# Other first loads, eleven products of zeros, one part per step at the start, and thirteen unread products before the feed-forward, in a one-layer decoder step

## The chip, the core and the metric

The kernel runs on one core of a Trainium2 chip. The metric is the device time of one execution in microseconds (us); lower is better. The engines meant below are TensorE (PE in the profile; its weight loads stand apart as PEld), VectorE (DVE), ScalarE (ACT), GpSimd (POOL) and the queue of SyncE (SP), which issues most of the transfers. A name such as ACTq or SPq is an engine's queue issuing a transfer.

## What is computed

One layer of a hybrid decoder over 288 token columns (256 of a prompt, 8 sequences of 4 new tokens), in fp32:

```python
h = _rmsnorm(x, norm_pre_mix)
z = h @ w_in                                   # 2048 -> 8480
ya, new_wkv = _rwkv7_branch(zs_mix, st_wkv, ...)
yb, new_pool = _pool_branch(zp, st_pool, pos0, pool_w, pool_scale)
m = sigmoid(zga) * (ya @ w_branch_a) + sigmoid(zgb) * (yb @ w_branch_b)
x = x + _rmsnorm(m @ w_out, norm_post_mix)
f, new_conv = _conv_ffn(_rmsnorm(x, norm_pre_ffn), ...)   # 2048 -> 2*5632 -> 2048
x = x + _rmsnorm(f, norm_post_ffn)
```

`_rmsnorm` divides each token's row by the root of its mean square and multiplies by a gain per channel.

## The kernel before

Activations lie with channels on the 128 partitions and the 288 tokens along the free dimension, so x is 16 tiles `xr` of 128x288. Every large product is made of three TensorE products in a fast 32-bit form (`three`, L262 to L265): the weights are split into a rounded part `whi` (a copy on ScalarE, L202) and the rest `wlo` (a subtraction on VectorE, L203), the activation into `xh` (ScalarE, L356) and `xl` (VectorE, L357), and hi·xh, hi·xl and lo·xh are added up in one PSUM bank. A **unit** is 128 output channels by 512 input channels of weights, one 256 KB load into one of seven `raw` buffers; it feeds 4 x 3 = 12 products. `whi` and `wlo` have four buffers each. `take` splits three units ahead of the one it hands out and loads six further.

**The beginning.** The RMS norm is not applied to x first: the products run on x times the gain, and the token's factor `rstd_mix` is multiplied in when a PSUM bank is read. The first group (`dense_together`, list `seq_lo`) works on five outputs at a time, one of them 96 channels wide: for each of four quarters of the input channels, five units, so 20 units and 240 products; units 0 to 4 need `xh` and `xl` of tiles 0 to 3, units 5 to 9 those of tiles 4 to 7, and so on. `startup` is a generator that runs beside it on a lane, one step per unit: it makes the parts of tiles 4 to 15, squares all tiles on ScalarE (`acc`, `sq`, L409 and L412), adds the squares on GpSimd (L413), and ends with `rstd_of`: a product with a tile of ones (L371), a square root and a reciprocal. `vec` holds all per-channel vectors (331 columns, gain g1 in the first 16), `con` the constants (1115 columns, with `ident`, `ones` and `bones`).

**The turn.** After the last of the 16 outputs of w_out, `rstd_spread` forms the norm of the mixed branch: six products with two columns of ones each (L384), a square root (L389), a reciprocal (L390), a diagonal tile (L392) and one product that spreads the factor over all partitions (L396). Then `second_parts` makes the new x tile by tile (L1229, L1230) and its parts, and the first three gate/up pairs of the feed-forward (`dense_by_k`, six outputs at a time) start, one tile k at a time in the first quarter and two at a time later. `rstd_spread` is called a second time at the end of the program, there with products for the residual sum in its pauses.

**What sets the order.** The program is recorded in the order of the code and then put into an order per engine by a scheduler that runs its own model of the engines' times; every engine executes its list strictly in that order. `pin` fixes an instruction's place among the pinned ones. A change in one place can therefore move instructions in others.

## Time and profile before

| | |
|---|---|
| median of 3 runs | 1649.15 us (1648.79 to 1650.57) |
| the profiled execution | 1651.69 us |
| its span, first to last instruction | 1649.6 us |
| mean granted TensorE clock | 0.992 |
| TensorE busy | 1611.8 us, 13540 products |
| VectorE, ScalarE, GpSimd busy | 1103.4, 816.8, 369.7 us |

The profile is of one execution. Its page gives busy times and the chain of work that ended last; the trace behind it answers by group of instructions, by wait (who stood still until whom), by time and by stretch of time (busy time of each engine, granted clock, transfer rate). "PE acc L263 <- ACT whi L202: 8.8, 1, 8.8" reads: TensorE's product of L263 waited for ScalarE's `whi` of L202, 8.8 us in all, once, 8.8 us the longest. In a timeline row stand start, length, engine, line, operation, out<-in, how many in a row, and in brackets the idle time before it and what ended that.

### The profile page before, as it was taken

The numbers are of one execution on the slowest core, as the hardware profiler recorded it, in microseconds if no ns is written. First come the engines' busy times: TensorE is split into PE (matmuls) and PEld (weight loads), VectorE is DVE, ScalarE is ACT, GpSimd is POOL, SyncE is SP. The second block draws the span as 40 slices with busy tenths as digits, with TensorE's granted clock in tenths as the row PEclk, the third lists the DMA queues.
The fourth block names the chain that finished last, engine by engine and source line by source line (L and its number), as shares of the span: only waits on it lengthen the run. The fifth ranks groups of instructions, "written<-read, shape, count | busy, mean of one in ns | idle before, by whom it ended". The sixth has DMA issues, their size and how long they took to land.

```text
span 1649.6 us, 35997 instructions
## 1 busy us (share of the span) xinstructions
PE 1611.8 (98%) x13540; PEld 1577.3 (96%) x13540; DVE 1103.4 (67%) x2217; ACT 816.8 (50%) x1521; POOL 369.7 (22%) x612
## 2 busy tenths in 40 slices
PE   6989999999999999999999999999999999999998
PEld 6989989989989999999899999999999999999998
DVE  6788887888878766645876664446666555666654
ACT  5544445445435445545655554445555433455554
POOL 4574352343332112300211110001111000111111
PEclk9999999999999999999999999999999999999999
DMA  7535546546545648755355555555555555555553
GB/s 241 161 120 165 170 142 200 161 122 190 157 155 181 187 155 288 229 166 190 108 163 167 167 165 167 166 167 165 168 167 166 166 166 167 166 167 167 176 167 108
DMA packets 157230, 278.96 MB, mean 169 GB/s; under 512 B 25584, under 2 KB 32240, under 8 KB 157056
## 3 DMA queue, kind: packets, MB, share of 16 engines
q1 hardware_dynamic: 151104, 259.16, 50.8%
q0 software_dynamic: 5664, 16.77, 2.9%
q8 instruction: 106, 1.74, 0.4%
q10 hardware_dynamic: 288, 0.74, 0.1%
q14 instruction: 68, 0.56, 0.1%
HBM read 262.67 MB, written 13.93 MB: 168 GB/s over the span
## 4 chain that ended last, share of the span: by engine, by line
PE 86%; DVE 4%; DMA 2%; issue 1%; POOL 0%; ACT 0%; SPq 0%; DVEq 0%; POOLq 0%; ACTq 0%
PE acc L265 27%; PE acc L263 27%; PE acc L264 27%; DVE wlo L203 1%; DMA dW<-wt 1%; PE ps_g L671 0%; DVE xl L357 0%; DVE og L1229 0%; PE ps_s L909 0%; DMA W<-dW 0%; PE ps_u L899 0%; PE ps_x L888 0%; PE ps_y L1353 0%; DVE cum L577 0%; DMA raw<-in_w_in 0%
## 5 line engine op out<-in xcount | busy, mean ns | idle before, releaser
L203 DVE TENSOR_TENSOR wlo<-raw,whi 128x512 fp32r<-128x512 f32 x928 | 661.1, 715 | 415.2 <-ACT whi L202 406.7
L202 ACT CAST whi<-raw 128x512 fp32r<-128x512 f32 x928 | 572.0, 620 | 680.6 <-PE acc L264 629.7
L263 PE MATMUL acc<-xh,whi 128*128 128x288 f32 x2736 | 814.3, 298 | 14.5 <-ACT whi L202 8.8
L265 PE MATMUL acc<-xh,wlo 128*128 128x288 f32 x2736 | 811.4, 297 | 7.0 <-DVE wlo L203 7.0
L264 PE MATMUL acc<-xl,whi 128*128 128x288 f32 x2736 | 812.7, 297 | 0.0
L263 PEld LDWEIGHTS acc<-xh,whi 128*128 128x128 f32 x2736 | 517.4, 189 | 17.9 <-ACT whi L202 9.2
L265 PEld LDWEIGHTS acc<-xh,wlo 128*128 128x128 f32 x2736 | 520.2, 190 | 12.0 <-DVE wlo L203 8.9
L264 PEld LDWEIGHTS acc<-xl,whi 128*128 128x128 f32 x2736 | 520.6, 190 | 2.0 <-issue 0.9
L265 PE MATMUL acc<-ah,wlo 128*128 128x288 f32 x704 | 208.7, 296 | 0.0
L263 PE MATMUL acc<-ah,whi 128*128 128x288 f32 x704 | 208.0, 296 | 0.0
L264 PE MATMUL acc<-al,whi 128*128 128x288 f32 x704 | 205.2, 292 | 0.0
L1266 POOL COPY cout<-gt 128x2 f32<-128x2 f32 x44 | 31.1, 706 | 597.2 <-DVE gt L1262 575.9
L264 PEld LDWEIGHTS acc<-al,whi 128*128 128x128 f32 x704 | 134.2, 191 | 0.0
L263 PEld LDWEIGHTS acc<-ah,whi 128*128 128x128 f32 x704 | 132.2, 188 | 0.0
L265 PEld LDWEIGHTS acc<-ah,wlo 128*128 128x128 f32 x704 | 131.9, 187 | 0.0
L1274 POOL TENSOR_TENSOR cv<-cv,rstd_ffn 128x288 f32<-128x288 f32 x44 | 36.2, 823 | 74.5 <-ACT cv L1273 73.6
L732 DVE TENSOR_TENSOR wt<-wt,Ab 128x16 f32<-128x16 f32 (+30 forms) x124 | 51.4, 414 | 1.8
L462 POOL TENSOR_TENSOR df<-zt 128x256 f32<-128x256 f32 (+1 forms) x27 | 22.7, 840 | 91.6 <-DVE zt L460 85.6
L1270 DVE SCALAR_TENSOR_TENSOR cv<-gt,vec,cv 128x255 f32<-128x255 f32 x88 | 43.0, 489 | 0.0
L263 PE MATMUL acc<-ybh,whi 128*128 128x288 f32 x128 | 38.6, 301 | 0.0
L265 PE MATMUL acc<-ybh,wlo 128*128 128x288 f32 x128 | 38.4, 300 | 0.0
L264 PE MATMUL acc<-ybl,whi 128*128 128x288 f32 x128 | 38.1, 298 | 0.0
(308 smaller groups left out, 1539.8 us busy)
## 6 DMA issues: line engine op xcount, KB each, us to landing
raw<-in_w_ffn_in SPq DMA_DIRECT2D x352, 256.0 KB, 3.0
raw<-in_w_in SPq DMA_DIRECT2D x264, 256.0 KB, 3.5
raw<-in_w_ffn_out SPq DMA_DIRECT2D x176, 256.0 KB, 2.7
raw<-in_w_out SPq DMA_DIRECT2D x64, 256.0 KB, 3.0
raw<-in_w_branch_b SPq DMA_DIRECT2D x32, 256.0 KB, 3.2
raw<-in_w_branch_a SPq DMA_DIRECT2D x32, 256.0 KB, 3.9
xr<-in_xT SPq DMA_DIRECT2D x8, 288.0 KB, 5.6
tga<-th POOLq DMA_DIRECT2D x16, 144.0 KB, 3.7
```

What stands on the lines that cost most here:

```text
L202: act.copy(out=hi[:, a:b, :m], in_=w[:, a:b, :m])
L203: dve.tensor_tensor(lo[:, a:b, :m], w[:, a:b, :m], hi[:, a:b, :m].bitcast(F32), op=ALU.subtract)
L263: pe.matmul(ps, hi, xh, start=start, stop=False)
L264: pe.matmul(ps, hi, xl, start=False, stop=False)
L265: pe.matmul(ps, lo, xh, start=False, stop=stop)
L462: pool.tensor_tensor(df[:m, :TP], zt[:m, 0:TP], zt[:m, 1:ZB], op=ALU.subtract)
L732: dve.tensor_tensor(tmp[:, :, :n], Wb[:, :, :n], Ab[:, :n, tt].unsqueeze(1).to_broadcast([P, 8, n]), op=ALU.mult)
L1266: pool.tensor_copy(cout[:, f, 0:2], gt[:, TP - 2:TP])
L1270: dve.scalar_tensor_tensor(cv[:, s:TP], gt[:, 0:TP - s], w, cv[:, s:TP], op0=ALU.mult, op1=ALU.add)
L1274: pool.tensor_tensor(cv, cv, rst3, op=ALU.mult)
```

## The change

Three things change at the beginning. The ScalarE queue now loads only the 16 columns of g1; the other 315 columns of `vec` and all of `con` are issued on the SP queue just before the load of unit 7. The first load of x brings one tile instead of two, then come unit 0, the second tile, and tiles 2 and 3. `startup` makes one tile's parts and one square per step, in pinned order of the squares. GpSimd zeroes a 128x128 tile, and eleven products of this tile with itself (plain fp32, `ps_warm`, read by nobody) stand first on TensorE. At the turn `rstd_spread` gets five products of `ones` with `ident` (`ps_busy`, read by nobody) behind the sums and eight behind the spreading product. `bones_r`'s copy is pinned. The second call of `rstd_spread` is as before.

```diff
+WARM = 11
@@ load_to
+            if i == 7:
+                nc.sync.dma_start(out=vec[:, KD:], in_=t["vec"][:, KD:])
+                nc.sync.dma_start(out=con, in_=t["con"])
@@
-    nc.scalar.dma_start(out=vec, in_=t["vec"])
+    nc.scalar.dma_start(out=vec[:, 0:KD], in_=t["vec"][:, 0:KD])
...
-    nc.scalar.dma_start(out=con, in_=t["con"])
@@ x_load
-            nc.sync.dma_start(out=xq[:, 0:2], in_=t["xT"][:, 0:2, :])
+            nc.sync.dma_start(out=xq[:, 0:1], in_=t["xT"][:, 0:1, :])
             nc.sync.dma_start(out=raw[0][:, 0:4], in_=units[0][0][:, 0:4])
+            nc.sync.dma_start(out=xq[:, 1:2], in_=t["xT"][:, 1:2, :])
             nc.sync.dma_start(out=xq[:, 2:4], in_=t["xT"][:, 2:4, :])
@@
+    def keep_busy(n):
+
+        ps = psb.tile([P, 512], F32, tag="s", name="ps_busy")
+        for _ in range(n):
+            pin(pe.matmul(ps[:, 0:P], ones, ident, start=True, stop=True))
+
-    def rstd_spread(sums, where, between=()):
+    def rstd_spread(sums, where, between=(), busy=()):
...
+        if busy:
+            keep_busy(busy[0])
...
         pin(pe.matmul(pr[:, :N], ones[0:TC], dg.rearrange("p c t -> p (c t)"), start=True, stop=True))
+        if busy:
+            keep_busy(busy[1])
@@ startup
-        for k in range(4, KD, 2):
-            first_parts(k)
-            first_parts(k + 1)
+        for k in range(KD):
+            if k < KD - 4:
+                first_parts(k + 4)
+            first_squares(k)
             yield
-        for k in range(KD):
-            first_squares(k)
-            if k % 2:
-                yield
@@
+    zero = xr_p.tile([P, P], F32, name="zero")
+    pool.memset(zero, 0.0)
+    warm0 = psb.tile([P, 512], F32, tag="s", name="ps_warm")
+    for _ in range(WARM):
+        pin(pe.matmul(warm0[:, :P], zero, zero, start=True, stop=True))
@@
-    act.copy(out=bones_r, in_=c_("bones"))
+    pin(act.copy(out=bones_r, in_=c_("bones")))
@@
-    rst2 = rstd_spread([acc2, sq], ep)
+    rst2 = rstd_spread([acc2, sq], ep, busy=(5, 8))
```

The order of the built programs follows at three places. First, what ScalarE executes at the very beginning, before:

```order
L320 DMA vec<-in_vec 128x331
L323 ACT_TABLE_LOAD
L323 ACTIVATE first<-first 128x1
L324 DMA con<-in_con 128x1115
L409 ACTIVATE acc_131<-xr_87 128x288
L412 ACTIVATE sq<-xr_87 128x288
L356 ACTIVATE xh_132<-xr_87,vec 128x288
L356 ACTIVATE xh_140<-xr_87,vec 128x288
L202 CAST whi<-raw 128x512
```

and with the change (lines are those of the changed file: L360 is L356 before, L206 is L202):

```order
L324 DMA vec<-in_vec 128x16
L327 ACT_TABLE_LOAD
L327 ACTIVATE first<-first 128x1
L360 ACTIVATE xh_148<-xr_86,vec 128x288
L206 CAST whi<-raw 128x512
L360 ACTIVATE xh_156<-xr_86,vec 128x288
L360 ACTIVATE xh_160<-xr_86,vec 128x288
L360 ACTIVATE xh_164<-xr_86,vec 128x288
L206 CAST whi<-raw 128x512
```

The two squares and the load of `con` are gone from the front, and unit 0's `whi` stands behind one `xh` instead of two.

Second, VectorE's list from the parts of tiles 6 and 7 on, before:

```order
L357 SCALAR_TENSOR_TENSOR xl_209<-xr_98,vec,xh_208 128x288
L357 SCALAR_TENSOR_TENSOR xl_213<-xr_98,vec,xh_212 128x288
L203 TENSOR_TENSOR wlo<-raw,whi 128x512 x3
L203 TENSOR_TENSOR wlo<-raw,whi 128x4x96
L357 SCALAR_TENSOR_TENSOR xl_233<-xr_111,vec,xh_232 128x288
L357 SCALAR_TENSOR_TENSOR xl_237<-xr_111,vec,xh_236 128x288
L357 SCALAR_TENSOR_TENSOR xl_257<-xr_111,vec,xh_256 128x288
L357 SCALAR_TENSOR_TENSOR xl_261<-xr_111,vec,xh_260 128x288
L357 SCALAR_TENSOR_TENSOR xl_281<-xr_124,vec,xh_280 128x288
L357 SCALAR_TENSOR_TENSOR xl_285<-xr_124,vec,xh_284 128x288
L357 SCALAR_TENSOR_TENSOR xl_305<-xr_124,vec,xh_304 128x288
L357 SCALAR_TENSOR_TENSOR xl_309<-xr_124,vec,xh_308 128x288
```

and with the change, from the weights of unit 4 on:

```order
L207 TENSOR_TENSOR wlo<-raw,whi 128x512 x3
L207 TENSOR_TENSOR wlo<-raw,whi 128x4x96
L207 TENSOR_TENSOR wlo<-raw,whi 128x512
L361 SCALAR_TENSOR_TENSOR xl_291<-xr_113,vec,xh_290 128x288
L361 SCALAR_TENSOR_TENSOR xl_314<-xr_113,vec,xh_313 128x288
L361 SCALAR_TENSOR_TENSOR xl_337<-xr_113,vec,xh_336 128x288
L361 SCALAR_TENSOR_TENSOR xl_362<-xr_113,vec,xh_361 128x288
L207 TENSOR_TENSOR wlo<-raw,whi 128x512 x2
L361 SCALAR_TENSOR_TENSOR xl_387<-xr_126,vec,xh_386 128x288
L361 SCALAR_TENSOR_TENSOR xl_412<-xr_126,vec,xh_411 128x288
L361 SCALAR_TENSOR_TENSOR xl_437<-xr_126,vec,xh_436 128x288
L361 SCALAR_TENSOR_TENSOR xl_462<-xr_126,vec,xh_461 128x288
```

Where eight parts (tiles 8 to 15) stood in a row ahead of the `wlo` of units 8 and later, unit 8 now comes ahead of all of them, and units 9 and 10 stand between the two groups of four.

Third, TensorE's list at the turn with the change:

```order
L394 MATMUL ps_sum<-con,acc_10057 96x2 x3
L394 MATMUL ps_sum<-con,sq 96x2 x3
L387 MATMUL ps_busy<-con 128x128 x5
L408 MATMUL ps_spread<-dg,con 128x288
L387 MATMUL ps_busy<-con 128x128 x8
L267 MATMUL acc<-xh_11342,whi 128x288 x6
```

Before, the three kinds `ps_sum`, `ps_spread` and `acc` stood there without the two `ps_busy` rows. On VectorE the list behind the turn moves too; after the parts of tile 9 it now goes on with weights:

```order
L361 SCALAR_TENSOR_TENSOR xl_11506<-x_10051,vec,xh_11505 128x288
L1247 TENSOR_TENSOR og_11056<-og_11056,ps_spread 128x288
L207 TENSOR_TENSOR wlo<-raw,whi 128x512 x2
L1248 TENSOR_TENSOR x_10053<-x_10053,og_11056 128x288
L207 TENSOR_TENSOR wlo<-raw,whi 128x512 x2
L361 SCALAR_TENSOR_TENSOR xl_11515<-x_10051,vec,xh_11514 128x288
```

where before two more tiles' parts (10 and 11) came ahead of the first `wlo`:

```order
L357 SCALAR_TENSOR_TENSOR xl_11475<-x_10035,vec,xh_11474 128x288
L1229 TENSOR_TENSOR og_11040<-og_11040,ps_spread 128x288
L357 SCALAR_TENSOR_TENSOR xl_11484<-x_10035,vec,xh_11483 128x288
L1229 TENSOR_TENSOR og_11040<-og_11040,ps_spread 128x288
L1230 TENSOR_TENSOR x_10037<-x_10037,og_11040 128x288
L357 SCALAR_TENSOR_TENSOR xl_11490<-x_10035,vec,xh_11489 128x288
L1229 TENSOR_TENSOR og_11040<-og_11040,ps_spread 128x288
L203 TENSOR_TENSOR wlo<-raw,whi 128x512 x2
```

So four `wlo` have moved ahead of the parts of tiles 10 and 11.

More of the change, by code (lines that the diff above doesn't have):

```diff
@@ L408, in first_squares @@
         if k == 0:
-            act.activation(out=acc, in_=xr[0], func=AF.Square)
+            pin(act.activation(out=acc, in_=xr[0], func=AF.Square))
             return
         sq = xr_p.tile([P, N], F32, tag="sq", name="sq", bufs=3)
-        act.activation(out=sq, in_=xr[k], func=AF.Square)
+        pin(act.activation(out=sq, in_=xr[k], func=AF.Square))
         pool.tensor_tensor(acc, acc, sq, op=ALU.add)
     def startup():
-        for k in range(4, KD, 2):
-            first_parts(k)
-            first_parts(k + 1)
+        for k in range(KD):
+            if k < KD - 4:
+                first_parts(k + 4)
+            first_squares(k)
             yield
-        for k in range(KD):
-            first_squares(k)
-            if k % 2:
-                yield
         norms["mix"] = rstd_of([acc], "mix", cst)
+    zero = xr_p.tile([P, P], F32, name="zero")
[3 more added lines that the diff above has]
+        pin(pe.matmul(warm0[:, :P], zero, zero, start=True, stop=True))
     first_parts(0)
```

## Prediction

> **What bounds the kernel now.** I read the page's head and its chain of work first.
>
> ```profile
> span 1649.6 us, 35997 instructions
> PE 1611.8 (98%) x13540; PEld 1577.3 (96%) x13540; DVE 1103.4 (67%) x2217; ACT 816.8 (50%) x1521; POOL 369.7 (22%) x612
> PE 86%; DVE 4%; DMA 2%; issue 1%; POOL 0%; ACT 0%; SPq 0%; DVEq 0%; POOLq 0%; ACTq 0%
> ```
>
> TensorE sets the end nearly everywhere, so only its standstills and its slow clock can be won. Next, who it waited for, over the whole span:
>
> ```profile
> PE acc L263 <- ACT whi L202: 8.8, 1, 8.8
> PE acc L265 <- DVE wlo L203: 7.6, 6, 3.3
> PE acc L263 <- DVE zb L1027: 4.1, 1, 4.1
> PE acc L263 <- ACT xh L356: 1.6, 1, 1.6
> ```
>
> The first and most of the second lie in the first 50 us; the fourth is the turn; the third lies elsewhere and is not touched directly. Groups of the first 50 us:
>
> ```profile
> L263 PE MATMUL acc<-xh,whi 128*128 128x288 f32 (+1 forms) x81 | 25.4, 316 | 8.8 <-ACT whi L202 8.8
> L265 PE MATMUL acc<-xh,wlo 128*128 128x288 f32 (+1 forms) x80 | 24.7, 317 | 4.7 <-DVE wlo L203 4.7
> L203 DVE TENSOR_TENSOR wlo<-raw,whi 128x512 fp32r<-128x512 f32 (+1 forms) x22 | 15.9, 750 | 9.6 <-ACT whi L202 8.7 <-DMA raw<-in_w_in 0.8
> L202 ACT CAST whi<-raw 128x512 fp32r<-128x512 f32 (+1 forms) x23 | 13.2, 596 | 15.5 <-PE acc L264 13.2 <-DMA raw<-in_w_in 2.2
> L357 DVE SCALAR_TENSOR_TENSOR xl<-xr,vec,xh 128x288 fp32r<-128x288 f32 x16 | 12.9, 865 | 1.5 <-ACT xh L356 1.5
> L356 ACT ACTIVATE xh<-xr,vec 128x288 fp32r<-128x288 f32 x16 | 7.6, 524 | 0.7 <-DMA xr<-in_xT 0.7
> ```
>
> 80 products of each kind by 50 us are the 240 of the first group; it ends at about 49.8. Now its time line:
>
> ```profile
> 1.19 0.42 SPq L333 DMA_DIRECT2D raw<-in_w_in  x1
> 8.16 0.62 ACT L202 CAST whi<-raw 128x512 fp32r<-128x512 f32 x1 [2.22 <-DMA raw<-in_w_in]
> 8.83 0.61 PE L263 MATMUL acc<-xh,whi 128*128 128x288 f32 x1 [8.83 <-ACT whi L202]
> 9.97 0.44 PE L263 MATMUL acc<-xh,whi 128*128 128x288 f32 x1
> 10.21 0.44 PE L264 MATMUL acc<-xl,whi 128*128 128x288 f32 x1
> 18.90 0.40 PE L265 MATMUL acc<-xh,wlo 128*128 128x288 f32 x1 [1.39 <-DVE wlo L203]
> 21.68 6.80 DVE L357 SCALAR_TENSOR_TENSOR xl<-xr,vec,xh 128x288 fp32r<-128x288 f32 x8
> 29.14 0.47 PE L265 MATMUL acc<-xh,wlo 128*128 128x288 f32 x1 [3.30 <-DVE wlo L203]
> ```
>
> Unit 0 lands 7.0 us after its issue; products then start every 0.24 us. Eight `xl` in a row keep the `wlo` of later units back, TensorE stands 3.30 us, and the clock falls, as the stretches of 1 us show (the column after POOL is the granted clock):
>
> ```profile
> 31.00:32.00 1.00, 1.00 (x6) 1.00 (x5) 0.00 (x0) 0.44 (x1) 0.00 (x0) 0.50 0.89 250
> 33.00:34.00 1.00, 1.00 (x10) 1.00 (x9) 0.00 (x0) 0.51 (x1) 0.00 (x0) 1.00 1.08 342
> ```
>
> The turn:
>
> ```profile
> 787.89 0.67 PE L384 MATMUL ps_sum<-con,sq 128*96 128x2 f32 x6 [0.45 <-ACT sq L1197]
> 789.60 0.75 PE L396 MATMUL ps_spread<-dg,con 96*128 96x288 f32 x2 [1.04 <-DVE dg L392]
> 791.96 1.81 PE L263 MATMUL acc<-xh,whi 128*128 128x288 f32 x6 [1.61 <-ACT xh L356]
> 793.57 0.44 PE L264 MATMUL acc<-xl,whi 128*128 128x288 f32 x1
> 793.81 0.44 PE L265 MATMUL acc<-xh,wlo 128*128 128x288 f32 x1
> 797.64 0.29 PE L264 MATMUL acc<-xl,whi 128*128 128x288 f32 x1
> 797.77 0.29 PE L265 MATMUL acc<-xh,wlo 128*128 128x288 f32 x1
> 790.00:791.00 1.00, 0.35 (x2) 0.00 (x0) 0.57 (x2) 0.00 (x0) 0.00 (x0) 0.75 0.25 84
> 797.00:798.00 1.00, 1.00 (x8) 1.00 (x8) 1.00 (x4) 0.00 (x0) 0.90 (x1) 0.84 0.00 0
> ```
>
> At half clock the products come every 0.24 us and last 0.44; at full clock every 0.13 (I use 0.131) and 0.29. So the products at 9.97 ran at half clock too.
>
> **Earlier first product: -2.9 us.** Two rows on loads (size, median us from issue to landing):
>
> ```profile
> con<-in_con ACTq DMA_DIRECT2D x1, 557.5 KB, 7.5
> raw<-in_w_in SPq DMA_DIRECT2D x264, 256.0 KB, 3.5
> ```
>
> Unit 0 took 7.0 us where such a load takes 3.5; beside it ran 557.5 KB of `con` and the whole of `vec`. Both now stand 12 issues behind on SP. I let unit 0 land between 1.2 + 3.5 = 4.7 and 5.3 us; the cast adds 0.6, so its first product could run at 5.4 to 6.0. Ahead of it stand the eleven products of zeros. Their price comes from a plain fp32 product of 288 columns:
>
> ```profile
> 1641.06 0.65 PE L1339 MATMUL ps_y<-x,con 128*128 128x288 f32 x2
> 1641.55 0.65 PE L1353 MATMUL ps_y<-f,con 128*128 128x288 f32 x2
> ```
>
> 0.49 us from start to start, so 0.22 us for 128 columns, 0.44 at half clock: 11 x 0.44 = 4.8 us. They wait for a GpSimd memset and can hardly begin before 1.0 us, so they end at 5.8 to 6.3. I take 5.9 for the first real product: 8.8 - 5.9 = 2.9 (bounds 2.2 and 3.4). Splitting x's first load and moving the two squares cost nothing while unit 0 lands last; without that cover each square costs ScalarE about 0.4 us once.
>
> **Fewer standstills and no slow clock in the first group: -6.2 us.** Before, 240 products from 8.8 to 49.8 took 41.0 us; at 0.131 they need 31.5, and the sum's product 0.5. The 9.0 between are 4.7 of waits for `wlo`, two stretches of half clock of some 14 products each (2 x 14 x 0.11 = 3.1), and 1.2 of small gaps. With the change the work fits: 16 `xl` and 20 `wlo` take VectorE 16 x 0.865 + 20 x 0.75 = 28.8 us, ScalarE's casts and parts 20 x 0.6 + 16 x 0.52 = 20 plus its squares, both under 31.5. What remains comes from order: unit 0 is paced by tiles 1 to 3, whose `xl` follow at 0.6 to 0.87 where three products take 0.39 (about 0.8 us); unit 4's `wlo` stands behind four `xl` (about 0.8); unit 11's behind the last four (4 x 0.87 = 3.5, of which the lead of two units, 2 x 12 x 0.131 = 3.1, covers most, and ScalarE's waits for buffers take some back: 1.2). Together 2.8, so 9.0 - 2.8 = 6.2. Bounds: 9.0 (no wait), and 2 if the waits stay and only the first stretch of half clock goes. The late constants are a new wait: four small VectorE instructions on `vec` stand ahead of unit 4's `wlo`; twelve loads of about 2.9 MB precede it, which at the 342 GB/s above is some 8.5 us after about 3, near the time they are due. One us late would cost one us there; it is inside my 2.8.
>
> [...]
>
> **Lost again behind it: +1.2 us.** The first bank can be read only when the token's factor is there:
>
> ```profile
> 46.35 0.42 DVE L460 TENSOR_TENSOR zt<-acc,rstd_mix 128x256 f32<-128x256 f32 x1
> ```
>
> Before, this was 3.4 us ahead of the group's end at 49.8. The squares are still spread over all twenty units, so their last sum comes relative to TensorE later than before, and three banks are not enough to run on for long. Nothing lost is one bound, 3.5 (the lead and a little) the other; I take a third.
>
> **The turn: -2.0 us.** Five products last 5 x 0.22 = 1.1 us in a pause of 1.04, eight last 1.75 in one of 1.61: at full clock they delay at most 0.2. If they hold the clock, the products from 791.96 to 797.2, some 22 at 0.24, run at 0.131: 22 x 0.11 = 2.4 less, minus 0.2, minus 0.25 as the first `xl` is not ready sooner. VectorE would be next late; it is full behind the turn (third figure, 19.69 of 20) and has to bring the same work 2 us earlier:
>
> ```profile
> 800.00:820.00 20.00, 19.51 (x144) 18.83 (x143) 19.69 (x38) 14.40 (x32) 6.15 (x6) 1.00 0.44 136
> ```
> But four `wlo` now stand ahead of two tiles' parts, some 2 x 0.87 us earlier, which I let cover it. Bounds: -2.4, and +3.0 (the second rival).
>
> **New order elsewhere: 0.** The scheduler moved instructions between 60 and 640 us on all engines. One event there shows the price:
>
> ```profile
> 100.00:120.00 20.00, 15.33 (x119) 14.61 (x117) 17.00 (x32) 7.43 (x15) 17.12 (x25) 0.83 0.36 111
> ```
>
> 4.7 us of standstill (4.1 of it the wait for `zb` above) and 17% of 20 us at a lower clock, 3.4: about 8 us for one stall long enough to drop the clock. I see no reason for a sign; -5 to +8 are my bounds.
>
> Sum: -2.9 - 6.2 + 1.2 - 2.0 = -9.9. From the profiled execution's 1651.7 that gives 1641.8. That execution lies 2.5 above the median of the runs, 1649.15, so for the median I forecast **1639.3 us**.
>
> **Rivals.** (1) *VectorE is the bound of the first group.* For: its `xl` took 0.85 us each while GpSimd added squares (6.80 for eight), and one square per step keeps GpSimd busy beside it throughout. Against: the sum of 28.8 above. Then only 2.9 and one stretch of slow clock (1.5) come from the start: -4.4 - 2.0 = 1642.8. (2) *The products at the turn stand in the way.* If the clock has fallen by then, five last 2.2 and eight 3.5 us, in pauses of 1.04 and 1.61: +1.1 + 1.9, and the half clock stays: +3.0 for -2.0, so 1644.3. [...] Against: the fall came only at 790.5, after all pauses but the last. (3) *The gain does not get through.* The stage behind the first group hangs on VectorE's chain from 46.35 on, not on TensorE, and the first group merely ends early: -1.5 - 2.0 leaves 1645.7 or more. Against: soon after, VectorE itself waits for TensorE to fill a bank:
>
> ```profile
> 70.33 0.43 DVE L460 TENSOR_TENSOR zt<-acc,rstd_mix 128x256 f32<-128x256 f32 x1 [0.37 <-PE acc L265]
> ```
>
> (4) *The other side: the new order makes new stalls in the stage from 60 to 640 us.* Place: a `wlo` or the reading of a bank behind a long VectorE instruction, as in the stretch just quoted; price 8 us each. One more gives 1647.3, no change; from the second on the kernel is slower, 1655.3. For: the order changed on every engine. Against: around that very wait VectorE's list is nearly the old one.
>
> **How the numbers follow.** Chances: forecast 0.60 (its own range 1635 to 1643.5), rival 1 0.14, rival 2 0.07, rival 3 0.07, rival 4 0.12 (one stall 0.06, two 0.06). About 0.2%, 3.3 us, can be told from no change: faster means under 1645.8, slower over 1652.4. Faster: 0.60 + 0.14 + 0.06 (of rival 2, which ends near the bound) = 0.80; slower 0.06; the rest, 0.14, the same. The range runs from 1633 (the better bounds of the first group, or an old stall gone) to 1647.
>
> **What would show it.** First real product near 5.9 us; products every 0.13 us from then on; no wait over 3 us before 45 us; the first group over near 40.7; at the turn a granted clock of 1.00 from 790 to 798 and the first product on `xh` near 792. I am wrong if the first group ends after 44 us, if the clock at the turn falls, or if the waits between 60 and 640 us change by more than 5 us.

## The result, and the profile after

The changed kernel takes 1639.81 us (median of 4 runs, 1638.9 to 1640.89) against 1649.86 us for the kernel before (median of 4, 1648.79 to 1651.35): a ratio of 0.9939, with a 95% interval of 0.9922 to 0.9956, or 10 us less. The forecast was 1639.3 us. The total was met, but not by the terms it was added up from: the gain at the beginning came out smaller than forecast, the gain at the turn was nearly all lost again, and a stretch that was put at nothing gave almost half of the whole.

The page of the changed kernel, its head and the chain of work that ended last (shares of the span by engine):

```profile
span 1637.8 us, 36108 instructions
PE 1612.2 (98%) x13588; PEld 1576.7 (96%) x13588; DVE 1102.1 (67%) x2217; ACT 816.2 (50%) x1521; POOL 366.3 (22%) x613
PE 85%; DVE 6%; issue 2%; DMA 1%; POOL 0%; ACT 0%; DVEq 0%; SPq 0%; ACTq 0%; POOLq 0%
```

TensorE's busy time hardly moved (1611.8 before, 1612.2 now, with 48 more product records), while the span fell by 11.8. The profiled execution itself took 1639.97 us, beside 1651.69 before. So standstills went, and the rows on waits say which. Who TensorE waited for over the whole span (total, times, longest):

```profile
PE acc L267 <- DVE zb L1045: 6.3, 2, 5.4
PE ps_x L906 <- DVE S L933: 3.6, 2, 2.3
PE acc L269 <- DVE wlo L207: 3.1, 5, 1.3
PE acc L267 <- DVE gt L1280: 2.0, 1, 2.0
```

The wait of 8.8 for the first `whi` and the 1.6 for `xh` at the turn are gone, and `wlo` is down from 7.6 to 3.1. Three things are new: the wait for `zb` is longer (5.4 in place of 4.1), `S` stops TensorE twice (3.6 in place of 1.3), and there is a wait of 2.0 for `gt`, which did not exist before. The time line of the changed kernel shows where each lies:

```profile
1.00 4.67 PE L442 MATMUL ps_warm<-zero 128*128 128x128 f32 x22 [1.00 <-POOL zero L439]
6.14 0.40 PE L267 MATMUL acc<-xh,whi 128*128 128x288 f32 x1 [0.46 <-ACT whi L206]
...
28.19 0.40 PE L269 MATMUL acc<-xh,wlo 128*128 128x288 f32 x1 [1.31 <-DVE wlo L207]
38.64 0.65 PE L375 MATMUL ps_rstd<-acc,con 128*128 128x288 f32 x2
40.33 0.41 ACT L367 CAST lo_h<-lora 128x256 fp32r<-128x256 f32 x1 [2.33 <-DMA lora<-in_lora]
42.05 0.50 ACT L377 ACTIVATE rstd_mix<-ps_rstd,con 128x288 f32<-128x288 f32 x1
42.59 1.95 DVE L378 RECIPROCAL rstd_mix<-rstd_mix 128x288 f32<-128x288 f32 x1 [1.39 <-ACT rstd_mix L377]
449.76 0.25 ACT L912 COPY X<-ps_x 128x128 f32<-128x128 f32 x1
776.29 0.59 PE L394 MATMUL ps_sum<-con,acc 128*96 128x2 f32 x6
779.64 1.95 PE L387 MATMUL ps_busy<-con 128*128 128x128 f32 x16
781.41 1.06 PE L267 MATMUL acc<-xh,whi 128*128 128x288 f32 x6
784.19 0.96 PE L267 MATMUL acc<-xh,whi 128*128 128x288 f32 x6
820.21 1.82 DVE L207 TENSOR_TENSOR wlo<-raw,whi 128x512 fp32r<-128x512 f32 x3
822.55 0.37 PE L267 MATMUL acc<-xh,whi 128*128 128x288 f32 x1 [2.00 <-DVE gt L1280]
```

Read from the top: the zeros run 4.67 us; the first real product comes at 6.14 in place of 8.83, and from 9.7 on products start every 0.13 us, but for the waits for `wlo` at 15.5 and 28.2. The first group ends with the product that starts at 42.46, in place of 49.75. Behind it `rstd_mix` is late: its sum is there at 39.3, but ScalarE stands until 40.33 for the load of `lora`, a weight that the next stage needs, and the square root (with 1.28 us of loading its table) stands behind that cast. In the kernel before, `lora` was issued at 31.3 and cast at 35.6, well ahead of the square root at 43.40; in the changed one it is issued at 36.2. At the turn the unread products fill the pauses. Forty microseconds later three `wlo` run ahead of `gt`, and TensorE waits.

The granted clock (third figure from the end, ahead of the share of DMA and the GB/s) at the turn, of the kernel before:

```profile
780.00:800.00 20.00, 16.89 (x109) 0.83 0.32 105
```

and of the changed kernel, with the stretch behind the first group:

```profile
44.00:46.00 2.00, 1.47 (x11) 1.00 0.00 0
780.00:800.00 20.00, 19.98 (x153) 1.00 0.23 70
```

To compare kernels, four marks cut each profiled execution: the first real product; the first product on `ybh` (the second big stage of the mixing half); the first `ps_sum` (the turn); the first product on `ah` (the first output of the feed-forward). The real work that TensorE does up to each mark is the same in all kernels but `zb` first (marked), except that the three with two sums have one more product with ones behind the turn; from `ah` to the end all take 650.0 to 650.2 us. All numbers in us.

| kernel | first product | to ybh | ybh to turn | turn to ah | median |
|---|---|---|---|---|---|
| before | 8.83 | 204.6 | 582.2 | 212.6 | 1649.86 |
| turn alone (same order up to the turn) | 7.85 | 202.3 | 582.2 | 211.4 | 1649.37 |
| loads alone | 6.01 | 198.9 | 582.7 | 211.8 | 1646.02 |
| steps alone | 8.15 | 201.5 | 584.1 | 211.9 | 1651.04 |
| changed | 6.14 | 197.6 | 578.7 | 211.4 | 1639.81 |
| changed, no products at the turn | 6.38 | 197.9 | 577.7 | 212.4 | 1640.29 |
| changed, no zeros | 6.50 | 197.5 | 580.9 | 213.0 | 1641.79 |
| changed, old steps | 6.32 | 198.7 | 583.5 | 213.0 | 1647.24 |
| changed, rstd ahead of lora | 6.40 | 196.1 | 578.7 | 213.0 | 1639.97 |
| the same, two sums behind the turn | 6.11 | 195.9 | 580.0 | 211.3 | 1639.51 |
| changed, zb first | 6.46 | 198.1 (128 products fewer) | 586.6 (128 more) | 213.0 | 1650.30 |
| changed, squares early | 6.25 | 201.1 | 577.3 | 212.9 | 1640.41 |
| the same, every third square apart | 6.28 | 198.0 | 578.7 | 210.9 | 1640.14 |
| changed, every fourth square apart | 6.46 | 198.5 | 576.6 | 210.4 | 1639.03 |

Each row is one execution, and some are executions of one order up to the turn: the first two; the changed kernel, the one without its turn and the last one; the two with the root ahead of `lora`; the two with the squares early. So the scatter of a stretch is known: up to 3 us as far as `ybh` (201.1 and 198.0), 2 us in the stretch behind it. A difference below that between two rows shows nothing. Taking the means of the first two executions and of the three of the changed order, the change won 5.5 us up to `ybh` (203.5 to 198.0) and 4.5 us from there to the turn (582.2 to 577.7).

What the second gain is made of can be read from that stretch in the kernel before, the changed one and the last one (start and end, length, TensorE's busy time):

```profile
204.61:786.84 582.23, 573.47 (x5610) 0.99 0.57 180
197.55:776.29 578.74, 573.03 (x5610) 0.99 0.58 181
198.49:775.09 576.60, 571.06 (x5611) 1.00 0.58 182
```

Length less busy time is standstill: 8.8 us before (8.5 in the other execution of that order), 5.7, 5.7 and 5.5 in the three of the changed order. So 3.0 of the 4.5 are standstill. The other 1.5 are products that ran faster (the granted clock in the rows is 0.99, 0.99 and 1.00), and this share changes from execution to execution of one order (573.0 to 571.1 busy).

### The profile page after: what moved, and what is told of

The parts are those of the page before. It is cut to its first block, busy times and chain, and to the rows that moved or that the text cites. A ratio compares the mean times of both kernels' runs of the same rounds, so it can differ in the third digit from the quotient of the medians.

```text
span 1637.8 us, 36108 instructions
## 1 busy us (share of the span) xinstructions
PE 1612.2 (98%) x13588; PEld 1576.7 (96%) x13588; DVE 1102.1 (67%) x2217; ACT 816.2 (50%) x1521; POOL 366.3 (22%) x613
## 4 chain that ended last, share of the span: by engine, by line
PE 85%; DVE 6%; issue 2%; DMA 1%; POOL 0%; ACT 0%; DVEq 0%; SPq 0%; ACTq 0%; POOLq 0%
PE acc L267 27%; PE acc L269 27%; PE acc L268 26%; DVE wlo L207 2%; DVE wt L750 1%; DVE wt L753 1%; PE ps_g L689 1%; DMA dW<-wt 0%; PE ps_x L906 0%; PE ps_s L927 0%; PE ps_x L907 0%; PE ps_y L1371 0%; DVE cum L595 0%; PE ps_u L917 0%; PE ps_st L858 0%
## 5 line engine op out<-in xcount | busy, mean ns | idle before, releaser
L206 ACT CAST whi<-raw 128x512 fp32r<-128x512 f32 x928 | 571.7, 619 | 669.0 <-PE acc L268 614.3
L1292 POOL TENSOR_TENSOR cv<-cv,rstd_ffn 128x288 f32<-128x288 f32 x44 | 35.6, 811 | 75.2 <-ACT cv L1291 74.4
L1288 DVE SCALAR_TENSOR_TENSOR cv<-gt,vec,cv 128x255 f32<-128x255 f32 (+1 forms) x88 | 43.0, 489 | 0.3 <-ACT cv L1281 0.3
```

The costliest lines, as they stand in the source:

```text
L206: act.copy(out=hi[:, a:b, :m], in_=w[:, a:b, :m])
L1288: dve.scalar_tensor_tensor(cv[:, s:TP], gt[:, 0:TP - s], w, cv[:, s:TP], op0=ALU.mult, op1=ALU.add)
L1292: pool.tensor_tensor(cv, cv, rst3, op=ALU.mult)
```

## The experiments

**The products at the turn, taken away and alone.** The first kernel is the changed one without them, the second the kernel before with them and nothing else. The edit of the first, and the core of the second in reverse:

```diff
-    rst2 = rstd_spread([acc2, sq], ep, busy=(5, 8))
+    rst2 = rstd_spread([acc2, sq], ep)
```

> The changed kernel without the thirteen unread products at the turn; its instructions stand in the same order up to the turn. Theory (the products hold the clock, and most of it is given back 40 us later, where rstd_ffn is late): the first ps_sum at the same time as in the changed kernel (776.3 +-0.7); the granted clock falls as it did before, and the first product of the second tile group comes 10.8 us behind the first ps_sum in place of 8.7; the wait of 2.0 us for gt is gone, since here gt follows the reciprocal directly; the first product on ah comes 212.6 us behind the first ps_sum in place of 211.4, and the whole takes about 1.2 us longer than the changed kernel (1641.0). Rival A (nothing is given back, the wait for gt comes from elsewhere): the wait stays and the whole takes 2.1 to 2.4 us longer (1642). Rival B (the products at the turn bring nothing): 1639.8.

> The kernel before with the thirteen unread products at the turn and nothing else; same order up to the turn. Theory: the first ps_sum at 786.8 +-0.7 as before, granted clock 1.00 from 787 to 800, the first product of the second tile group 8.7 us behind the first ps_sum in place of 10.8; three wlo stand between the reciprocal of rstd_ffn and gt, so a wait of about 2 us for gt at about 833 appears; the whole is 1.0 to 1.3 us shorter than before (1648.5). Rival A (no gt wait without the earlier start): 2.1 to 2.4 shorter. Rival B: no shorter at all.

Measured: without them 1640.29 us (0.9941 of before, 0.9923 to 0.9959), alone 1649.37 us (0.9998, 0.9989 to 1.0008). Time line of the changed kernel without them:

```profile
775.65 0.59 PE L394 MATMUL ps_sum<-con,acc 128*96 128x2 f32 x6
784.79 0.96 PE L267 MATMUL acc<-xh,whi 128*128 128x288 f32 x6
819.16 0.46 DVE L1280 TENSOR_TENSOR gt<-acc,rstd_ffn 128x288 f32<-128x288 f32 x1 [1.52 <-PE acc L269]
```

Time line of the kernel before with them:

```profile
784.48 0.59 PE L390 MATMUL ps_sum<-con,acc 128*96 128x2 f32 x6
792.37 0.96 PE L263 MATMUL acc<-xh,whi 128*128 128x288 f32 x6
830.13 0.81 DVE L1272 TENSOR_TENSOR gt<-acc,rstd_ffn 128x288 f32<-128x288 f32 x2
```

The next tile group's first six `whi` products come 7.9 us behind the first sum with the unread products in both kernels (792.37 - 784.48, and 784.19 - 776.29), 9.1 and 9.6 without them (the changed kernel without them, and the kernel before): they win 1.2 to 1.7 us there. In these four kernels the wait for `gt` comes and goes with them. Without them `gt` runs straight behind the reciprocal, is ready before TensorE, and waits for it (1.52); with them the scheduler puts three `wlo` between, and TensorE waits 2.0. At `ah` 0.9 to 1.1 is left of the gain, and that only in these two executions; the loads alone and the steps alone, without unread products, took 211.8 and 211.9 there, so part of it lies within the scatter. In five others with the same wait (no zeros, old steps, rstd first, zb first, squares early) the clock fell behind it, as in the line of the fourth experiment below (0.91 from 820 to 840), and `ah` came 212.9 to 213.0 behind the first sum, later than without any unread products. So the theory holds with its places, and the sum is smaller than it said: over all runs the turn moved the whole by less than can be told (0.5 us in one pair of medians, 0.2 in the other), which by the total alone is also what the rival had that gives the products no worth.

**No zeros.** The changed kernel without the tile of zeros and its eleven products.

```diff
-    zero = xr_p.tile([P, P], F32, name="zero")
-    pool.memset(zero, 0.0)
-    warm0 = psb.tile([P, 512], F32, tag="s", name="ps_warm")
-    for _ in range(WARM):
-        pin(pe.matmul(warm0[:, :P], zero, zero, start=True, stop=True))
```

> The changed kernel without the eleven products of zeros; all else at the beginning in the same order. Both theories: the first real product at 6.1 as in the changed kernel (it waits for unit 0's cast, which starts at 5.5), and the first 3.4 to 7 us of products at half clock (every 0.24 us in place of 0.13), so 14 to 28 products by 0.11 = 1.6 to 3.1 us more to do at the start; the waits for wlo at 15.5 and 28.2 (1.9 together) may take part of it back. The first group ends at 43 to 45 in place of 42.4. Theory L (the end of the first group is not what sets the next stage, but rstd_mix, ready at 44.55): the first product on ybh comes less than 1 us later than in the changed kernel (197.5), the whole 0 to 1 us longer. Rival (TensorE's end of the group sets the next stage): 1.6 to 3 us longer at the first ybh and at the end (1641.4 to 1643).

Measured: 1641.79 us (0.9952, 0.9937 to 0.9967). Its time line:

```profile
6.50 0.61 PE L267 MATMUL acc<-xh,whi 128*128 128x288 f32 x1 [6.50 <-ACT whi L206]
39.41 0.65 PE L375 MATMUL ps_rstd<-acc,con 128*128 128x288 f32 x2
197.49 0.29 PE L267 MATMUL acc<-ybh,whi 128*128 128x288 f32 x1
```

Products start every 0.24 us from 6.5 to about 12.2, then every 0.13. The sum for `rstd_mix`, at the same place in TensorE's list, comes 0.8 us later than in the changed kernel (39.41 for 38.64), 0.4 of it by the later start; the wait for `wlo` at 15.5, which is absent here, takes the rest of the slow products back. By `ybh` nothing of it is left (197.49 for 197.55). So theory L, as far as one execution with a scatter of 1 to 3 us can show it: the zeros bring the clock up (with them products start every 0.13 us from 9.7 on), and little of what they win passes the group. The whole is 2 us longer, as the rival had it, but not at the rival's place: the profiled execution loses it behind `ybh`, where from 322 us on this kernel's lists on VectorE and ScalarE stand in another order, and behind the wait for `gt`.

**The square root ahead of lora's cast.** In the changed kernel the square root and the cast are held in program order, the square root first.

```diff
-        exact_parts(lo_h, lo_l, lora)
+        exact_parts(lo_h, lo_l, lora, True)
...
-        act.activation(out=r, in_=ps[:, :N], func=AF.Sqrt, scale=1.0 / D, bias=c_("eps"))
+        rt = act.activation(out=r, in_=ps[:, :N], func=AF.Sqrt, scale=1.0 / D, bias=c_("eps"))
+        if name == "mix":
+            pin(rt)
```

> The changed kernel with the square root of rstd_mix held ahead of the cast of lora on ScalarE, where it stood behind it and waited for lora's load until 40.3. Theory L: the square root runs at about 40 in place of 42.05 (the sums are there at 38.6, and 1.28 go to the table), the reciprocal starts at 40.5 in place of 42.6 and ends at 42.5, level with the end of the first group; the stall of about 1.4 us of TensorE at 44 to 46 goes; the first ybh comes 1 to 2 us earlier than 197.5. Rival (VectorE and the load of lora set this stage, not the factor): the stall only moves to ps_w, and the first ybh stays within 0.5 us of 197.5. Behind that the order of instructions differs on all engines, so the whole can go either way by up to 4 us.

Measured: 1639.97 us (0.9943, 0.9929 to 0.9958). Stretches of this kernel, then its time line:

```profile
0.00:10.00 10.00, 8.01 (x36) 0.93 0.81 242
10.00:20.00 10.00, 10.00 (x70) 0.90 1.05 381
820.00:840.00 20.00, 18.92 (x131) 0.91 0.35 112
```

```profile
40.36 1.95 DVE L380 RECIPROCAL rstd_mix<-rstd_mix 128x288 f32<-128x288 f32 x1 [1.13 <-ACT rstd_mix L377]
196.08 0.29 PE L267 MATMUL acc<-ybh,whi 128*128 128x288 f32 x1
```

The reciprocal starts 2.2 us earlier (40.36 for 42.59), TensorE no longer stands at 44 to 46, and `ybh` comes 1.5 to 2.4 us earlier than in the three executions of the changed kernel's order (195.9, as early, in the second execution of this one), although in this execution the clock fell from 8.6 to 12.0 in spite of the zeros (0.93 and 0.90). Theory L again, with two reserves: a scatter of up to 3 us was seen at this mark, and behind 49 us the lists stand in another order too, so not all of the 2 us need be the factor's. The whole is no shorter: in this execution 1.5 us went again behind the wait for `gt`, where the clock fell (third line).

**The loads alone, the steps alone, the change with the old steps.** Before plus the new loads; before plus one part and one square a step; the changed kernel with the old steps. The core of the second, and of the third in reverse:

```diff
-        for k in range(4, KD, 2):
-            first_parts(k)
-            first_parts(k + 1)
-            yield
         for k in range(KD):
+            if k < KD - 4:
+                first_parts(k + 4)
             first_squares(k)
-            if k % 2:
-                yield
+            yield
```

> The kernel before with the new loads alone: x's first tile by itself ahead of unit 0, the late part of vec and con behind seven units on SP. The parts and squares stay in the old order, and there are no zeros. The old order gave the first real product at 8.83 and at 7.85 in two executions, and the first product on ybh at 204.6 and 202.3. Theory D (the loads bring the first product, the steps bring the missing standstills): first real product at 6.1 to 6.6, the stretch of half clock at the beginning stays, the eight xl in a row and the wait for wlo behind them (1.6 to 3.3 us) stay; first ybh 1.4 to 2.5 us earlier than the old order, 200 to 202.5. Rival E (the early loads carry all of the 5 to 7 us): first ybh at 197.5. Rival F (an earlier beginning only meets a longer wait for wlo): first ybh at 202 to 204.6, nothing won. Behind that the order differs a little, so the whole may go either way by 4 us.

> The kernel before with one part and one square a step alone; old loads, no zeros. Theory D: first real product at 7.8 to 8.8 as before, half clock for the first 5 to 8 us as before, no wait for wlo over 1.5 us behind it and no second stretch of half clock; first ybh 3 to 4.5 us earlier than the old order's 202.3 to 204.6, so 198 to 201. Rival E: no gain, 202.3 to 204.6. Rival G (steps carry it all): 197.5 although the first product comes 2 us later than in the changed kernel.

> The changed kernel with the old order of parts and squares (two parts a step, the squares behind all parts, not pinned), so new loads, zeros and the products at the turn. The loads alone gave a first ybh at 198.9, the steps alone 201.5, the old order 202.3 to 204.6, the whole change 197.5 to 197.9. Theory M (the loads carried nearly all, the zeros some 1.5 us, the steps nothing or less): first real product at 6.1 to 6.5, half clock absent or short, rstd_mix at 33 to 36 and no stall behind the group; first ybh at 196.5 to 198. Rival (the steps are worth the 3 us that they brought beside the old loads): eight xl in a row bring a wait for wlo of over 2 us back, first ybh at 199.5 to 201. The whole depends on the order further on, 1636 to 1645.

Measured: loads alone 1646.02 us (0.9979, 0.9970 to 0.9989), steps alone 1651.04 us (1.001, 1.000 to 1.0019), the change with the old steps 1647.24 us (0.9988, 0.9979 to 0.9997). Time line of the loads alone:

```profile
6.01 0.61 PE L266 MATMUL acc<-xh,whi 128*128 128x288 f32 x1 [6.01 <-ACT whi L205]
29.18 0.40 PE L268 MATMUL acc<-xh,wlo 128*128 128x288 f32 x1 [1.05 <-DVE wlo L206]
198.92 0.29 PE L266 MATMUL acc<-ybh,whi 128*128 128x288 f32 x1
```

Up to `ybh` the loads alone win 3.4 to 5.7 us of the change's 5.5 (against the two executions of the old order): the first product comes at 6.01, and with the new order on SP the scheduler also breaks up the eight `xl` of VectorE's list, so that the longest wait for `wlo` in the first group is 1.07 without any change to the steps. In the old order it was 3.30 in one execution and 1.62 in the other. In the steps alone the eight `xl` still stand in a row, with a wait of 1.78 behind them; they win 0.9 to 3.2 up to `ybh`. With the loads in place the old steps (198.7, between that run's two forecasts) are within the scatter of the new (197.6 to 198.5). Rival E, the loads, had the mechanism nearly right; of my theory the share of the steps falls.

Yet without the steps the change is worth 2 to 2.6 us of 10, which neither theory had expected. Of the 7.4 that are missing, the profiled executions show 1.1 up to `ybh`, 1.5 behind the wait for `gt` (the clock fell), and 4.8 where no line was edited, between `ybh` and the turn: 583.5 with the old steps, 576.6 to 578.7 with the new. In the kernel before there is a wait in that stretch that goes a long way to explain it:

```profile
456.13 0.44 ACT L1099 ACTIVATE th<-th 128x288 f32<-128x288 f32 x1 [2.34 <-DVE th L1096]
456.48 0.25 ACT L894 COPY X<-ps_x 128x128 f32<-128x128 f32 x1
456.78 0.69 PE L899 MATMUL ps_u<-X,W 64*64 64x64 f32 x8 [2.81 <-ACT X L894]
```

On VectorE `th` (L1096) stands behind a part of `AR`, a `wlo` of 1.76 and a `KB`; on ScalarE `X` stands behind `th`'s tanh; TensorE waits 2.81 for `X`. In the changed kernel `X` follows the copies of `W` directly at 449.76 (row above), and TensorE's wait for it is gone. The kernels divide by this wait: it is 2.3 to 2.9 in before, turn alone, loads alone, steps alone and with the old steps, with 582.2 us or more from `ybh` to the turn; it is 0.4 or absent in eight others, with 580.9 or less. (`zb` first has it too, but its stretch holds other work.) That is a correlation over 13 executions, not an edit that takes this wait alone away; its length is close to the 3.0 us of standstill above, and what it costs beside its length was not measured apart. TensorE's wait for it in the change with the old steps, between 200 and 770 us:

```profile
PE ps_u L920 <- ACT X L915: 2.8, 1, 2.8
```

**zb first.** The changed kernel with the `KB` products of the first pair of heads two slots later.

```diff
         yield lambda: g == 0 or g - 1 in past
+        if g == 0:
+            yield 2
```

> The changed kernel with the four KB products of the first pair of heads (one on VectorE of 1.64, two on GpSimd of 1.7 each stand at that place) two slots later, so that on VectorE the fourth zb no longer stands behind one; same order up to that place. Theory (rival 4's price: a stall ahead of zb costs its own length and a stretch of half clock behind it): the wait of 5.4 us for zb at 101 falls to 2.5 to 3.5 us (the two wlo ahead of it, 1.2 each, get shorter without GpSimd beside them), the granted clock in 90 to 110 rises from 0.86 and 0.79 to 0.95 or more, and the first ybh comes 2.5 to 4.5 us earlier than 197.5. Rival (what zb waits for is only moved: the KB products are then late for the next stage): the first ybh comes earlier, but the first ps_sum stays within 1 us of 776.3, and the whole at 1639.8.

Measured: 1650.30 us (1.0003, 0.9994 to 1.0013), the whole gain lost. TensorE's waits of this kernel between 50 and 200 us:

```profile
PE acc L267 <- DVE zb L1047: 3.6, 1, 3.6
PE acc L267 <- DVE wt L755: 3.3, 1, 3.3
```

The wait for `zb` fell from 5.4 to 3.6, less than forecast, one of 3.3 for `wt` came, and from about 99 us on the order of the lists changed, with the wait for `X` back. `ybh` cannot be compared here, but the first sum of the turn came at 784.6, 8 us later than in the changed kernel; neither theory nor rival had expected it later. This is the fourth rival's mechanism, a new order with other stalls, made by an edit that takes no work away and adds none. The loss is as large as the price the rival put on one stall, but it is not one stall: no single wait here is over 3.6 us, and which parts make up the 8 us was not taken apart.

**The squares early.** The last four squares in two steps.

```diff
-            yield
+            if k < KD - 4 or k % 2:
+                yield
```

> The changed kernel in which the last four squares go into two steps in place of four, so that the sum for rstd_mix stands 13 rows earlier on TensorE; from the end of the first group on, the instructions stand almost everywhere as in the changed kernel, so this changes the first group alone. Theory L (rstd_mix, held up by the late end of the squares and by lora's load behind it, is what the stage behind the first group waits for): ps_rstd at 36.5 to 37.5 in place of 38.6, the reciprocal starts at 40.5 to 41.5 in place of 42.6, the stall of 0.5 to 1.4 us at 44 to 46 goes, first ybh at 195.5 to 197 in place of 197.5 and 197.9, and the whole 1 to 2 us shorter than the changed kernel (1638 to 1639). Rival (VectorE, loaded with two squares' sums more in those steps, delays wlo): nothing won, 197.5 to 198.5, and 1639.8.

Measured: 1640.41 us (0.9951, 0.9939 to 0.9963): nothing won. Its time line:

```profile
37.16 0.65 PE L375 MATMUL ps_rstd<-acc,con 128*128 128x288 f32 x2
40.79 0.41 ACT L367 CAST lo_h<-lora 128x256 fp32r<-128x256 f32 x1 [4.14 <-DMA lora<-in_lora]
45.60 0.40 PE L269 MATMUL acc<-xh,wlo 128*128 128x288 f32 x1 [1.49 <-DVE wlo L207]
```

The sum came 1.5 us earlier (37.16 for 38.64), and it helped nobody, since ScalarE then stood 4.14 us for `lora`, whose load landed no earlier (40.79 for 40.33), with the square root and four `whi` behind it. In a second execution of this order up to the turn (the kernel with every third square apart) the load landed earlier:

```profile
39.46 0.41 ACT L367 CAST lo_h<-lora 128x256 fp32r<-128x256 f32 x1 [2.78 <-DMA lora<-in_lora]
```

There the reciprocal began at 41.71, against 43.05 in the first, with the sum at the same place (37.19): the factor follows `lora`'s landing and not the squares. In theory L that part falls. `ybh` came at 201.1 and 198.0, later in the first than both forecasts; there the clock fell from 46.3 to 49.7 behind the wait of 1.49 for `wlo` at 45.60; the second is like the changed kernel. So neither shows a gain, and 0.9 us on the reciprocal alone is less than this mark can tell.

**Two sums behind the turn, in three shares.** Half of the squares of the second norm (with the square root ahead of `lora`), a third (with the squares early) and a quarter (in the changed kernel itself) are summed by GpSimd in a tile of their own. The edit of the last:

```diff
+        elif k == 1:
+            act.activation(out=acc3b, in_=x2[1], func=AF.Square)
         else:
             sq = square(x2[k])
-            dve.tensor_tensor(acc3, acc3, sq, op=ALU.add)
+            if k % 4 == 1:
+                pool.tensor_tensor(acc3b, acc3b, sq, op=ALU.add)
+            else:
+                dve.tensor_tensor(acc3, acc3, sq, op=ALU.add)
...
-        norms["ffn"] = rstd_of([acc3], "ffn", ep)
+        norms["ffn"] = rstd_of([acc3, acc3b], "ffn", ep)
```

> The previous experiment's kernel (the changed kernel with the square root of rstd_mix ahead of lora's cast) and, behind the turn, the squares of the second norm summed by VectorE and GpSimd half each into two tiles, which the product with ones adds up; same order up to the turn. Theory (at the turn 1.7 to 2.1 us are won, and then VectorE, late with rstd_ffn and three wlo ahead of gt, takes 2.0 back, and in executions where the clock falls behind that wait another 1.5): rstd_ffn starts 2 to 4 us earlier behind the first ps_sum (42.05 in the changed kernel), gt follows the reciprocal directly, no wait for gt; first ah 209.4 to 210.9 us behind the first ps_sum in place of 211.4 (212.9 in the executions where the clock fell), and the whole 0.5 to 3.5 us shorter than that kernel (1636.5 to 1639.5). Rival (GpSimd, which adds x2 there, becomes late in its place): the wait moves to xh or wlo of the second stage, and first ah stays at 211.4 to 213.

> The previous edit, and behind the turn every third square of the second norm summed by GpSimd into a tile of its own, with the two products with ones eight rows later on TensorE than in the experiment that summed half of them there; same order up to the turn as in the previous edit. Theory: no wait of 2.0 for gt and no wait of 1.4 for acc either; first ah 209.3 to 210.5 us behind the first ps_sum (211.4 in the changed kernel, 212.9 where the clock fell behind gt), the whole 1 to 2 us below the previous edit, 1636.5 to 1638. Rival (each repair moves the wait, since VectorE is full there): 211 to 212 behind the first ps_sum, and the previous edit's time.

> The changed kernel and, behind the turn alone, every fourth square of the second norm summed by GpSimd into a tile of its own; same order as the changed kernel up to the turn. The two products with ones now stand about 20 rows earlier on TensorE than the one in the changed kernel and 8 rows later than in the previous experiment, and one wlo stands between the reciprocal of rstd_ffn and gt in place of three. Theory (the wait for gt gives back what the products at the turn win, and can be had away): no wait for acc and none for gt, no fall of the clock in 820 to 840; first ah 209.3 to 210.0 us behind the first ps_sum in place of 211.4 or 212.9; the whole 1.4 to 2.5 us below the changed kernel, 1637.3 to 1638.4. Rival (VectorE is full there, each repair moves the wait): a wait of 0.5 to 1.5 remains, 210.5 to 211.5, and the whole within 1 us of the changed kernel's 1639.8.

Measured: half 1639.51 us (0.9940, 0.9925 to 0.9954), a third 1640.14 us (0.9949, 0.9937 to 0.9962), a quarter 1639.03 us (0.9933, 0.9921 to 0.9946). From the turn to `ah`: 211.3, 210.9 and 210.4. Time line of the first:

```profile
813.28 0.72 PE L375 MATMUL ps_rstd<-acc,con 128*128 128x288 f32 x2 [1.37 <-DVE acc L1264]
```

and of the last:

```profile
813.65 0.72 PE L375 MATMUL ps_rstd<-acc,con 128*128 128x288 f32 x2 [0.49 <-DVE acc L1264]
817.85 0.44 DVE L1286 TENSOR_TENSOR gt<-acc,rstd_ffn 128x288 f32<-128x288 f32 x1
```

In all three the wait for `gt` is gone, and with it the fall of the clock. In its place TensorE waits for the sums themselves, 1.4, 1.0 and 0.5 us: as the rival of the last two had it, the repair moves the wait, and a smaller one remains. In all three `ah` came later than the theory's range, by 0.4 us. In the stretch from the turn to `ah` the last is 1.1 to 2.6 us better than the kernels with the wait, and it has the lowest median of all. Its distance to the changed kernel, 0.8 us, is less than the runs can tell.

## Why the prediction was right, and where it was not

- **Earlier first product (-2.9).** Right in kind, and in the pair of profiles in size: 8.83 to 6.14, 2.7. Over all profiled executions it is 6.01 to 6.50 in the eleven with the new loads and 7.85 to 8.83 in the three with the old ones, so the mean gain is 2.0, below the lower bound of 2.2. Unit 0 landed at 5.47 rather than by 5.3, and its cast set the first product; the zeros, which the sum let end at 5.8 to 6.3, were over at 5.67.
- **Fewer standstills, no slow clock in the first group (-6.2).** The group ended 7.3 earlier, 2.7 of it by the start, so 4.6: 1.6 too much was forecast. The failed step is the waits that were kept. All three came at their places and each was larger: the pacing by tiles 1 to 3 cost 1.5 us between 6.1 and 9.7 (0.8 forecast), `wlo` at 15.5 1.0 (0.8), `wlo` at 28.19 1.5 (1.2), counted as what the starts lie further apart than 0.131, so 4.0 in place of 2.8; small gaps, for which the sum kept nothing, made another 0.5. The base was also too high: the 41.0 us from which the 9.0 were taken are one execution. The second execution of the old order took 39.0 for the same 240 products, with 1.62 in place of the wait of 3.30 and no fall of the clock behind it, so that in the means the group won 3.6 (40.0 to 36.4). What was wrong in kind is the cause: the eight `xl` go with the loads alone, and the zeros' 1.5 us hardly reach the group's end.
- **Lost again behind it (+1.2).** From the group's last product to `ybh` the old order took 154.9 and 155.4, the changed one 155.1 to 155.7: the stretch grew by 0.2 in the means, not by 1.2. There was something to win there, about 2 us by the two executions that moved the square root (198.0 to 196.0), but it was not lost against the kernel before. "The squares are still spread over all twenty units" was the wrong reason for the late factor: with the sum 1.5 us earlier nothing was won. It is `lora`'s load, in ScalarE's list ahead of the square root.
- **The turn (-2.0).** The first half of the step was right: clock 1.00, products every 0.13, 1.2 to 1.7 us won by the second tile group. The sentence that failed is "VectorE would be next late", followed by "which I let cover it": at the turn itself no new wait came, but three `wlo` more stand ahead of `gt`. The term was costed up to the next tile, and should have been costed up to `ah`. Net -1.1 at best, and +0.4 to +0.6 where the clock falls behind the new wait.
- **New order elsewhere (0, -5 to +8).** Inside the bounds, but it was -3.5 in the profiled executions and -4.5 in the mean, nearly half of the gain: an old stall, the wait for `X`, went. "I see no reason for a sign" was a fair answer to what the profile of before showed, and the experiments bear it out: the same work in this stretch came out at 576.6 to 584.1 with small edits.

Put together: forecast -7.9 up to the end of the first stage, -2.0 at the turn, 0 between; measured in the means -5.5, about 0 to -1, and -4.5. The sum is right because the third, put at nothing, made up for the first two. That the total came within 1 us is luck; what held is the first product, the clock at the turn and the places of the kept waits.

**The rivals.** The first (VectorE bounds the first group) has a size, -4.4, that lies nearer to the mean (-5.6 to the group's end) than the forecast's -9.1, but its mechanism falls: VectorE was busy for 27.1 of the group's 36.3 us, and TensorE's waits in it came from the order. The second (the products stand in the way) falls at its own place, since nothing was delayed at the turn; the loss 40 us later has another mechanism. The third (the gain does not get through) holds for the zeros alone. The fourth is a real mechanism: 8 us up to the turn in the kernel with `zb` first, 5 to 6 us between old and new steps. In this change its sign was the other one.

**What was to show it.** The first real product was to come near 5.9 (6.14), products every 0.13 us from then on (from 9.7), no wait of over 3 us before 45 (1.31 the longest behind the start), the group over near 40.7 (42.5, inside the limit of 44), the clock 1.00 behind the turn (it was), the waits between 60 and 640 us within 5 us of the old ones (TensorE stood 16.2 us there before, 13.5 now). "The first product on `xh` near 792" was badly put: it comes 5.1 us behind the first sum with or without the products, at 781.41, since all ahead of it had moved.

**The zeros and the clock.** The sum took the clock to be up behind the zeros in every execution, which was the author's assumption. Of nine profiled executions with the zeros it stayed up in seven (products every 0.13 us from about 10 us on); in two, the square root ahead of `lora` and `zb` first, it fell behind them (products every 0.24 us, a granted clock of 0.93 up to 10 us and of 0.90 from 10 to 20 us in both), in the one shown (the square root ahead of `lora`) from 8.6 to 12.0. What sets these two apart no run shows. On the spot that is some 14 products by 0.11, 1.5 us. Up to the group's end it was 0.2: in both the 240 products took 36.6 us from start to start, against 36.3 to 36.4 in the three of the changed order, since TensorE then no longer waits for `wlo` at 15.5.

## What to carry to other kernels

Where one engine is busy 98% of the span and a scheduler orders the rest, cost an edit up to the next stage's first product, not up to the end of the stall it removes: twice here (zeros, turn) a stall that went came back as a wait for what had been hidden behind it. Before calling a factor late because of its inputs, look at what stands ahead of it in its engine's list, above all a cast that waits for a load. And when an edit changes the scheduler's order far away, time the edit's parts alone as well as taken out: the loads alone gave 3.5 us, the steps alone cost 1.6 (interval 0 to 3), and all parts together gave 10, some 4.5 of it in a stretch that none of them touched, where the order that came out had one stall less.

## What the runs showed of the chip

- A wait of 2.0 us on TensorE, after 35 us of steady products, was followed by a fall of the granted clock in five executions of seven (0.91 from 820 to 840) and by none in two (1.00). The same wait thus costs 2.0 or about 3.5 us.
- The column of the granted clock does not show the clock of the very beginning: in the kernel without zeros the products run every 0.24 us up to 12.2, the spacing that goes with a granted clock of 0.50 elsewhere (at the turn of the kernel before), while these stretches read 1.00:

```profile
5.00:10.00 5.00, 3.50 (x12) 1.00 1.06 375
10.00:15.00 5.00, 5.00 (x32) 1.00 1.06 381
```

- The products of zeros ran at half clock for most of their length: 0.21 us a record, where the unread products at the turn took 0.11. The 22 records took 4.07 to 5.07 us over the nine executions, since in most of them the last few ran at 0.11; the first real products behind them ran at full clock (0.29 us long where no wait stood ahead, 0.40 behind one).
- One order of instructions, executed twice, reached the same product on `ybh` at 204.6 and 202.3: the start differed by 1 us (8.83 and 7.85) and the waits for `wlo` in the first group by 3.1 (4.7 and 1.6).
